# State-space decay exponents from running sums read back from HBM, in a hybrid diffusion trunk

## The chip, the cores and the metric

The kernel runs on one NeuronCore of a Trainium2 chip. Its engines work in parallel from instruction streams of their own: TensorE (PE, matrix products into PSUM), VectorE (DVE), ScalarE (ACT), GpSimd (POOL) and SyncE (SP, which here only issues DMAs). The metric is the device time of one execution in microseconds (us); lower is better. The time of the kernel before is the median of three runs, 1761.66 us (1760.66 to 1762.17).

## The reference

A two-layer trunk over 512 latent tokens of width 1024, with 256 context tokens. Layer 0 has a mixer of two parts, a Mamba-2 state-space group (SSD: 16 heads of 64 channels, two groups, state 128, both directions) and a gated linear attention group; layer 1 has a conformer convolution; both layers end in a convolutional gated MLP. The change lies in the SSD part, which for each direction computes, in chunks of 128 tokens:

```
a_cum = jnp.cumsum(a, -1)                       # a = dt * a_coef, per head
decay = jnp.exp(segsum(a))                      # exp(cs[l] - cs[s]) for s <= l, else 0
cb = jnp.einsum('bclgn,bcsgn->bgcls', cc, bc)
y_diag = jnp.einsum('bgcls,bgjcls,bcsgjp->bclgjp', cb, decay, xdt)
...
y = y_diag + y_off      # y_off: what the state at the chunk's start contributes
```

Here `xdt` is the token's value times its step size dt. The two directions are added, a skip term `d_skip * xs` comes on top, the result is multiplied by silu(z) and normalized by its root mean square in two groups of 512 channels. Inputs and weights are float32.

## The kernel before

The whole trunk is one program. Tokens lie on 128 partitions, four chunks of latent tokens and two of context. The weights are streamed in blocks of 128x512: `_wload` (L178) issues one DMA on SP (L182), ACT casts the upper half `whi` into the matmul's number format (L184), and the lower half `wlo = wraw - whi` is subtracted on DVE or, where `lo_pool` is set, on GpSimd (L188). Five blocks are loaded ahead. A projection then takes three matmuls per product: hi x hi, lo x hi, hi x lo (L214 to L216, L233 to L235).

The SSD stage is `mixer` with `dt_stage` (L510) and `ssd` (L592). `dt_stage` makes the step sizes `dt`, the decays `a`, and by matmuls with triangles of ones the running sums p1 and totals p2, whose exponentials are `ef` and `dtot`. `mixer` then runs, for each of two groups of eight heads, the convolution of that group's channels (`conv5`, L328 to L340), transposes into token order (`to_tokens`, L342), and `ssd`. The scheduler of the framework orders each engine's stream by priorities, so that matmuls of the next projections (`ps`, `psv`, `psz`) fall between those of the SSD loop; a change in the code thus moves other instructions too.

In `ssd`, after the backward states (`u`, `sb`) and the products `pcb = B C` of all four chunks, a loop runs over four chunks and in each over two halves of four heads:

- ACT multiplies the triangle masks by `a`, eight times 128x128 (`r`, L644); PE turns them into the decay exponents with two fp32 matmuls of 128x512 (`seg`, L645); ACT takes the exponential (`e`, L647).
- ACT and DVE make the weight `w`, which has both directions' dt times the masked products `cbm` (L633, L650, L651); DVE forms `e*w` (L653); four matmuls by head give `yp` (L656).
- The states' part is two matmuls `po` (L661), scaled on DVE into `yo` (L663). DVE adds skip, yp and yo into `y` and multiplies by silu(z) (L667 to L671). ACT squares and sums (L672); `sf` is carried on by `u` and DVE.

After the loop, DVE makes the root-mean-square factor in a chain of small operations (`rstd`, L588, L256 to L261) and scales `y` (L682). PSUM is shared by pools: four buffers `mm` for projections, two `lv` (seg, pcb), two `mi` (yp, po, u, transposes). A matmul into a new tile waits until the buffer's last reader is through. The attention part follows: its value projection `psv` is copied out by ACT into `v` (L496).

Of the kernel before, what the change touches and what calls it, by code (L numbers as in the profile page):

```python
# [8 lines left out]
F32 = mybir.dt.float32  # L9
F32R = mybir.dt.float32r  # L10
BF16 = mybir.dt.bfloat16
I32 = mybir.dt.int32
# [135 lines left out]
class Net:  # L148
# [193 lines left out]
    def to_tokens(self, src, dst, n, mi):  # L342

        nc = self.nc
        pt = mi.tile([P, n, P], F32, tag="mi", name="pt")
        for c in range(n):
            nc.tensor.transpose(pt[:, c, :], src[:, c * P:(c + 1) * P], self.ident)
        nc.scalar.copy(dst, pt)

    def mixer(self):  # L350
# [93 lines left out]
        sp = ss.enter_context(self.pool("ssp", 1))  # L444
        dx = self.stack()
# [3 lines left out]
        dt, a, ef, dtot, wdec = dts  # L449
        self.dump("dt", dt)  # L450
# [7 lines left out]
        for g in range(2):  # L458
# [4 lines left out]
            for i in range(4):  # L463
                ps, ps2 = self.fm(mm, "win", C_XS + (g * 4 + i) * P, act, also=actc)
                xf = self.conv5(ps, T, g * 4 + i, tmps)
                self.to_tokens(xf, y[:, :, (g * 4 + i) * P:(g * 4 + i + 1) * P], NCH, mi)
                xf2 = self.conv5(ps2, TC, g * 4 + i, tmps)
                self.to_tokens(xf2, xct[:, :, i * P:(i + 1) * P], NCC, mi)
# [4 lines left out]
            self.ssd(g, y, xct, bfm, cfm, btok, dts, rows, sz, sp, tmps, lv, mi)  # L473
# [38 lines left out]
    def dt_stage(self, act, actc, sp, sx, mm, mi, rows):  # L512
# [51 lines left out]
        dtot = sp.tile([P, 2, NC6, H], F32, name="dtot")  # L564
        nc.scalar.activation(out=ef, in_=p1, func=AF.Exp)
# [6 lines left out]
        return dt, a, ef, dtot, wdec  # L572
# [19 lines left out]
    def ssd(self, g, y, xct, bfm, cfm, btok, dts, rows, sz, sp, tmps, lv, mi):  # L592
        nc = self.nc
        dt, a, ef, dtot, wdec = dts
# [35 lines left out]
        cbm = sp.tile([P, 2, NCH, P], F32, tag="cbm", name="cbm")  # L630
        for d in range(2):
            m = (self.le, self.ge)[d]
            nc.vector.tensor_tensor(out=cbm[:, d], in0=pcb, in1=bass.AP(tensor=m.tensor, offset=m.offset, ap=[list(m.ap[0]), [0, NCH], [1, P]]), op=ALU.mult)  # L633
        ssq = tmps.tile([P, NCH], F32, tag="ssq", name="ssq")
        for c in range(NCH):
            yp = mi.tile([P, 512], F32, tag="mi", name="yp")
            for hq in range(2):
                h0 = g * GH + hq * 4
                r = tmps.tile([P, 2, 4, P], F32, tag="r", name="r", bufs=1)
                seg = lv.tile([P, 4, P], F32, tag="lv", name="seg")  # L640
                for d in range(2):
                    m = (self.le, self.ge)[d]
                    for j in range(4):
                        nc.scalar.mul(r[:, d, j, :], m, a[:, c, d, h0 + j:h0 + j + 1])  # L644
                    nc.tensor.matmul(seg, (self.gt, self.lt)[d], r[:, d], start=d == 0, stop=d == 1)  # L645
                e = tmps.tile([P, 4, P], F32, tag="e", name="e")
                nc.scalar.activation(out=e, in_=seg, func=AF.Exp)  # L647
                w = tmps.tile([P, 4, P], F32, tag="w", name="w")
                for j in range(4):
                    nc.scalar.mul(w[:, j, :], cbm[:, 1, c, :], dt[:, c, 1, h0 + j:h0 + j + 1])  # L650
                    nc.vector.scalar_tensor_tensor(out=w[:, j, :], in0=cbm[:, 0, c, :], scalar=dt[:, c, 0, h0 + j:h0 + j + 1],  # L651
                                                   in1=w[:, j, :], op0=ALU.mult, op1=ALU.add)
                nc.vector.tensor_tensor(out=e, in0=e, in1=w, op=ALU.mult)  # L653
# [12 lines left out]
            dd = rows[:, R_D - R_DTB + g * GH:R_D - R_DTB + (g + 1) * GH]  # L666
            nc.vector.tensor_tensor(out=heads(yc), in0=heads(yc), in1=bch(dd, HD), op=ALU.mult)  # L667
# [12 lines left out]
        for c in range(NCH):  # L680
            yc = y[:, c, g * 512:(g + 1) * 512]
            nc.vector.tensor_scalar_mul(yc, yc, r[:, c:c + 1])  # L682
# [567 lines left out]
```

## Time and profile before

| what | value |
|---|---|
| median of three runs | 1761.66 us |
| the profiled execution | 1762.31 us, span 1760.5 us |
| PE busy | 1707.3 us, 97% of the span |
| DVE busy | 1247.9 us, 71% |
| ACT busy | 850.5 us, 48% |
| POOL busy | 525.8 us, 30% |
| last links of the chain that ended last | PE lines L214 to L216 above all |

The profile gives for each engine the time in which it worked, and for each group of instructions count, sum and mean. A share over the whole span hides stages: GpSimd at 30% does nothing at all in the SSD stage, which lies at about 100 to 290 us of the span. So rows of that stretch count. In the timeline a row has start, length, engine, line, operation and tiles; the length of an instruction overlaps that of the next, so that distances from start to start, not lengths, are what a sequence costs.

### The profile page before, as it was taken

The numbers are of one execution on the slowest core, as the hardware profiler recorded it, in microseconds if no ns is written. First come the engines' busy times: TensorE is split into PE (matmuls) and PEld (weight loads), VectorE is DVE, ScalarE is ACT, GpSimd is POOL, SyncE is SP. The second block draws the span as 40 slices with busy tenths as digits, with TensorE's granted clock in tenths as the row PEclk, the third lists the DMA queues.
The fourth block names the chain that finished last, engine by engine and source line by source line (L and its number), as shares of the span: only waits on it lengthen the run. The fifth ranks groups of instructions, "written<-read, shape, count | busy, mean of one in ns | idle before, by whom it ended". The sixth has DMA issues, their size and how long they took to land. (4 is left out here: it accounts for less than half of the span.)

```text
span 1760.5 us, 26474 instructions
## 1 busy us (share of the span) xinstructions
PE 1707.3 (97%) x9574; PEld 1465.3 (83%) x9574; DVE 1247.9 (71%) x2368; ACT 850.5 (48%) x1713; POOL 525.8 (30%) x436
## 2 busy tenths in 40 slices
PE   6999999999999999999999999999999999999996
PEld 5987768989899987887888888988898888888886
DVE  7778988969695996378777731488788777776125
ACT  4556775354444544364333422499534743333233
POOL 4400000000000003544444444533415444444451
PEclk9999999999999999999999999999999999999998
DMA  9621102434343448423333333322203233333331
GB/s 365 239 66 48 31 19 89 135 119 154 109 144 120 133 139 277 134 85 114 108 108 108 109 112 96 102 73 60 61 26 90 85 96 98 100 96 96 96 107 61
DMA packets 92194, 194.02 MB, mean 110 GB/s; under 512 B 10496, under 2 KB 13568, under 8 KB 92064
## 3 DMA queue, kind: packets, MB, share of 16 engines
q1 hardware_dynamic: 92016, 192.21, 35.0%
q8 instruction: 75, 1.23, 0.3%
q14 instruction: 55, 0.45, 0.1%
q0 software_dynamic: 48, 0.13, 0.0%
HBM read 190.21 MB, written 2.10 MB: 109 GB/s over the span
## 5 line engine op out<-in xcount | busy, mean ns | idle before, releaser
L188 POOL TENSOR_TENSOR wlo<-wraw,whi 128x512 fp32r<-128x512 f32 x388 | 510.0, 1318 | 1188.5 <-ACT whi L184 1171.6
L184 ACT CAST whi<-wraw 128x512 fp32r<-128x512 f32 x488 | 300.9, 619 | 509.2 <-PE ps L215 254.0
L214 PE MATMUL ps<-h1hi,whi 128*128 128x512 f32 x768 | 299.9, 391 | 2.0 <-DVE acc L1066 1.9
L216 PE MATMUL ps<-h1hi,wlo 128*128 128x512 f32 x768 | 299.6, 390 | 0.6 <-POOL wlo L188 0.6
L215 PE MATMUL ps<-h1lo,whi 128*128 128x512 f32 x768 | 299.6, 390 | 0.0
L1066 DVE SCALAR_TENSOR_TENSOR acc<-ps,pcol,acc 128x441 f32<-128x441 f32 (+2 forms) x320 | 222.4, 695 | 57.5 <-ACT acc L1058 47.9
L214 PEld LDWEIGHTS ps<-h1hi,whi 128*128 128x128 f32 x768 | 144.5, 188 | 32.2 <-ACT acc L1058 2.3
L216 PEld LDWEIGHTS ps<-h1hi,wlo 128*128 128x128 f32 x768 | 144.6, 188 | 31.2 <-POOL wlo L188 1.1
L215 PEld LDWEIGHTS ps<-h1lo,whi 128*128 128x128 f32 x768 | 144.7, 188 | 29.5
L273 DVE CUSTOM_DVE_ANT_0 junk<-ada,sc,pcol 128x1024 bf16<-128x1024 f32 x80 | 105.8, 1322 | 14.8 <-DMA ada<-adaw 14.6
L903 DVE SCALAR_TENSOR_TENSOR x<-ps,mod,x 128x512 f32<-128x512 f32 x14 | 10.5, 750 | 146.7 <-PE ps L216 146.7
L215 PE MATMUL ps<-glo,whi 128*128 128x512 f32 x264 | 102.7, 389 | 0.0
L214 PE MATMUL ps<-ghi,whi 128*128 128x512 f32 x264 | 102.7, 389 | 0.0
L216 PE MATMUL ps<-ghi,wlo 128*128 128x512 f32 x264 | 102.7, 389 | 0.0
L1158 DVE SCALAR_TENSOR_TENSOR cr<-u,pcol,cr 128x511 f32<-128x511 f32 (+20 forms) x156 | 97.7, 699 | 1.7 <-ACT cr L1141 1.5
L214 PE MATMUL ps<-hhi,whi 128*128 128x512 f32 x240 | 98.0, 408 | 0.0
L215 PE MATMUL ps<-hlo,whi 128*128 128x512 f32 x240 | 96.5, 402 | 0.0
L216 PE MATMUL ps<-hhi,wlo 128*128 128x512 f32 x240 | 96.0, 400 | 0.0
L188 DVE TENSOR_TENSOR wlo<-wraw,whi 128x512 fp32r<-128x512 f32 x100 | 68.0, 686 | 26.0 <-ACT whi L184 25.2
L979 DVE TENSOR_TENSOR glo<-acc,ghi 128x512 fp32r<-128x512 f32 x44 | 56.4, 1282 | 29.7 <-ACT ghi L978 29.6
L233 PE MATMUL psz<-whi,hhi 128*128 128x256 f32 (+1 forms) x224 | 67.5, 302 | 0.0
L234 PE MATMUL psz<-wlo,hhi 128*128 128x256 f32 (+1 forms) x224 | 67.1, 300 | 0.0
(353 smaller groups left out, 4168.0 us busy)
## 6 DMA issues: line engine op xcount, KB each, us to landing
wraw<-wst SPq DMA_DIRECT2D x488, 256.0 KB, 2.7
ada<-adaw SPq DMA_DIRECT2D x104, 512.0 KB, 3.6
xk<-xT SPq DMA_DIRECT2D x8, 256.0 KB, 7.8
x<-xT SPq DMA_DIRECT2D x8, 256.0 KB, 5.1
out<-n SPq DMA_DIRECT2D x16, 128.0 KB, 1.7
xk<-ctxT SPq DMA_DIRECT2D x8, 128.0 KB, 4.0
sc<-rows SPq DMA_DIRECT2D x1, 512.0 KB, 3.5
scc<-rows SPq DMA_DIRECT2D x1, 512.0 KB, 7.6
```

The lines of the kernel that those rows point to most:

```text
L184: nc.scalar.copy(hi, raw)
L188: eng.tensor_tensor(out=lo, in0=raw, in1=hi.bitcast(F32), op=ALU.subtract)
L214: mm(ps, w[0], a[0], start=start, stop=False)
L215: mm(ps, w[0], a[1], start=False, stop=False)
L216: mm(ps, w[1], a[0], start=False, stop=stop)
L233: mm(ps, a[0], w[0], start=start, stop=False)
L234: mm(ps, a[0], w[1], start=False, stop=False)
L273: nc.vector.tensor_tensor_reduce(out=junk, in0=raw, in1=self.sc if cond is None else cond, scale=1.0, scalar=self.pc("adab", n), op0=ALU.m ...
L903: self.after = self.nc.vector.scalar_tensor_tensor(out=r, in0=ps, scalar=self.modc(layer, j, i), in1=r, op0=ALU.mult, op1=ALU.add)
L979: return nc.vector.tensor_tensor(out=lo, in0=x, in1=hi.bitcast(F32), op=ALU.subtract)
L1066: nc.vector.scalar_tensor_tensor(out=o, in0=grid(pg)[:, r0 + dy - 1:r1 + dy - 1, c0 + dx - 1:c1 + dx - 1], scalar=wcol(dy, dx), in1=o, op0 ...
L1158: nc.vector.scalar_tensor_tensor(out=acc[:, t0:t1], in0=u[:, t0 + d:t1 + d], scalar=self.pc("cdw", tap * 8 + i), in1=acc[:, t0:t1], op0=AL ...
```

## The change

The exponents no longer come from matmuls. `dt_stage` copies the running sums out of p1, transposes them on PE (`pcum`), copies them by ACT (`crow`) and writes them to a DRAM scratch `cumd` of 32 rows by 512 tokens with a DMA on ACT's queue. `nb` holds ln(dt) minus the running sum of the token on the partition. In `ssd` each (chunk, half) reads eight rows of `cumd`, each on all 128 partitions, 512 KB in pieces of 512 bytes, by ACT's queue into `r` (three buffers). ACT adds `nb` as a bias: direction 0 into `e` in SBUF, direction 1 into `seg` in PSUM. DVE copies the second over the first where the mask says "after" (copy_predicated), ACT takes one exponential, and DVE multiplies by the unmasked `cb`. The weight dt is thus in the exponent. The diagonal's second direction and the skip factor are put together in `own` (one reduction and one small operation per chunk). The scaling of `y` by the root-mean-square factor moves from DVE to ACT, and `lo_pool` is on from the end of `dt_stage` to the end of the second `ssd`.

```diff
+        self.cumd = ss.enter_context(self.pool("cumd", 1, bass.MemoryType.DRAM)).tile([2 * H, T], F32, name="cumd")
...
+        self.lo_pool = True
         for g in range(2):
...
-                self.to_tokens(xf2, xct[:, :, i * P:(i + 1) * P], NCC, mi)
+                done = self.to_tokens(xf2, xct[:, :, i * P:(i + 1) * P], NCC, mi)
...
+            self.ssd(g, y, xct, bfm, cfm, btok, dts, rows, sz, sp, tmps, lv, mi, done)
+        self.lo_pool = False
...
+        cum = sx.tile([P, NCH, H // 4, 2, 4], F32, name="cum")
+        by4 = lambda t: t.rearrange("p c (q j) -> p c q j", j=4)
+        for d in range(2):
+            nc.vector.tensor_copy(cum[:, :, :, d, :], by4(p1[:, d, 0:NCH, :]))
+        pcum = mi.tile([P, T], F32, tag="mi", name="pcum")
+        for c in range(NCH):
+            nc.tensor.transpose(pcum[:32, c * P:(c + 1) * P], cum[:, c].rearrange("p q d j -> p (q d j)"), self.ident)
+        crow = sx.tile([32, T], F32, name="crow")
+        nc.scalar.copy(crow, pcum[:32, :])
+        nc.scalar.dma_start(out=self.cumd, in_=crow)
+
+        nb = sp.tile([P, NCH, 2, H], F32, name="nb")
+        nc.vector.tensor_scalar_max(nb, dt[:, 0:NCH], 1e-30)
+        nc.scalar.activation(out=nb, in_=nb, func=AF.Ln)
+        for d in range(2):
+            nc.vector.tensor_tensor(out=by4(nb[:, :, d, :]), in0=by4(nb[:, :, d, :]), in1=cum[:, :, :, d, :], op=ALU.subtract)
...
-        cbm = sp.tile([P, 2, NCH, P], F32, tag="cbm", name="cbm")
-        for d in range(2):
-            m = (self.le, self.ge)[d]
-            nc.vector.tensor_tensor(out=cbm[:, d], in0=pcb, in1=bass.AP(tensor=m.tensor, offset=m.offset, ap=[list(m.ap[0]), [0, NCH], [1, P]]), op=ALU.mult)
+        cb = sp.tile([P, NCH, P], F32, tag="cb", name="cb")
+        nc.scalar.copy(cb, pcb)
+
+        own = sp.tile([P, NCH, GH], F32, tag="own", name="own")
+        cbd = sp.tile([P, NCH], F32, tag="cbd", name="cbd")
+        dd = rows[:, R_D - R_DTB + g * GH:R_D - R_DTB + (g + 1) * GH]
+        for c in range(NCH):
+            junk = tmps.tile([P, P], F32, tag="cj", name="cj", bufs=1)
+            nc.vector.tensor_tensor_reduce(out=junk, in0=cb[:, c, :], in1=self.ident, scale=1.0, scalar=0.0, op0=ALU.mult, op1=ALU.add,
+                                           accum_out=cbd[:, c:c + 1])
+            nc.vector.scalar_tensor_tensor(out=own[:, c, :], in0=dt[:, c, 1, g * GH:(g + 1) * GH], scalar=cbd[:, c:c + 1], in1=dd,
+                                           op0=ALU.mult, op1=ALU.add)
+        after = bass.AP(tensor=self.gt.tensor, offset=self.gt.offset, ap=[list(self.gt.ap[0]), [0, 4], [1, P]]).bitcast(I32)
...
-                r = tmps.tile([P, 2, 4, P], F32, tag="r", name="r", bufs=1)
+                r = tmps.tile([P, 2, 4, P], F32, tag="r", name="r", bufs=3)
+                cd = self.cumd[:]
+                nc.scalar.dma_start(out=r, in_=bass.AP(tensor=cd.tensor, offset=cd.offset + h0 * 2 * T + c * P, ap=[[0, P], [T, 8], [1, P]]))
+
+                e = tmps.tile([P, 4, P], F32, tag="e", name="e")
                 seg = lv.tile([P, 4, P], F32, tag="lv", name="seg")
-                for d in range(2):
-                    m = (self.le, self.ge)[d]
-                    for j in range(4):
-                        nc.scalar.mul(r[:, d, j, :], m, a[:, c, d, h0 + j:h0 + j + 1])
-                    nc.tensor.matmul(seg, (self.gt, self.lt)[d], r[:, d], start=d == 0, stop=d == 1)
-                e = tmps.tile([P, 4, P], F32, tag="e", name="e")
-                nc.scalar.activation(out=e, in_=seg, func=AF.Exp)
-                w = tmps.tile([P, 4, P], F32, tag="w", name="w")
-                for j in range(4):
-                    nc.scalar.mul(w[:, j, :], cbm[:, 1, c, :], dt[:, c, 1, h0 + j:h0 + j + 1])
-                    nc.vector.scalar_tensor_tensor(out=w[:, j, :], in0=cbm[:, 0, c, :], scalar=dt[:, c, 0, h0 + j:h0 + j + 1],
-                                                   in1=w[:, j, :], op0=ALU.mult, op1=ALU.add)
-                nc.vector.tensor_tensor(out=e, in0=e, in1=w, op=ALU.mult)
+                with self.tc.issue_after(done.ins):
+                    for d, dst in ((0, e), (1, seg)):
+                        for j in range(4):
+                            nc.scalar.activation(out=dst[:, j, :], in_=r[:, d, j, :], func=AF.Identity, bias=nb[:, c, d, h0 + j:h0 + j + 1])
+                nc.vector.copy_predicated(e, after, seg)
+                nc.scalar.activation(out=e, in_=e, func=AF.Exp)
+                nc.vector.tensor_tensor(out=e, in0=e, in1=ap(cb, c * P, [[0, 4], [1, P]]), op=ALU.mult)
...
-            nc.vector.tensor_tensor(out=heads(yc), in0=heads(yc), in1=bch(dd, HD), op=ALU.mult)
+            nc.vector.tensor_tensor(out=heads(yc), in0=heads(yc), in1=bch(own[:, c, :], HD), op=ALU.mult)
...
-            nc.vector.tensor_scalar_mul(yc, yc, r[:, c:c + 1])
+            nc.scalar.mul(yc, yc, r[:, c:c + 1])
```

The scheduler puts the new streams together anew. Three places matter here. Rows are instructions in the order of one engine: line, operation, written and read tiles with their numbers, shape, and how many alike follow each other. The lines are those of each version's own code.

On PE, at the end of the second group: before, the last chunk's yp and po matmuls are mixed with the value projection (psv).

```order
L656 MATMUL yp_2727<-y_84,e_2740 128x64 x4
L661 MATMUL po_2784<-sf_2723,cfm_100 128x512
L233 MATMUL psv_2963<-whi51_2360,chi_88 128x256
L656 MATMUL yp_2727<-y_84,e_2768 128x64 x4
L234 MATMUL psv_2963<-wlo51_2362,chi_88 128x256
L235 MATMUL psv_2963<-whi51_2360,clo_89 128x256
L233 MATMUL psv_2963<-whi51_2360,chi_88 128x256
L661 MATMUL po_2788<-sb_2442,cfm_100 128x512
L234 MATMUL psv_2963<-wlo51_2362,chi_88 128x256
```

After the change, the same place on PE (L683 is now yp, L688 po, L701 u):

```order
L701 MATMUL u_2640<-xd_2624,btok_101 128x512
L216 MATMUL ps_2919<-hhi_79,wlo53_2745 128x512
L683 MATMUL yp_2646<-y_84,e_2649 128x64 x4
L688 MATMUL po_2685<-sf_2642,cfm_100 128x512
L683 MATMUL yp_2646<-y_84,e_2668 128x64 x4
L688 MATMUL po_2689<-sb_2402,cfm_100 128x512
L214 MATMUL ps2_2920<-chi_88,whi52_2326 128x256
L215 MATMUL ps2_2920<-clo_89,whi52_2326 128x256
```

The value projection, and the latent half of the next projection (`ps_2919`), now stand ahead of the last chunk; its context half `ps2_2920` follows the last po directly.

On ACT, at the same place, before: the last exponentials, four casts of weights, the last square and sum, then the copies of the value projection.

```order
L647 ACTIVATE e_2768<-seg_2757 128x512
L184 CAST whi54_2847<-wraw54_2845 128x512
L184 CAST whi55_2853<-wraw55_2851 128x512
L184 CAST whi56_2859<-wraw56_2857 128x512
L184 CAST whi57_3021<-wraw57_3019 128x512
L672 ACTIVATE yo_2790,ssq_2489<-y_84 128x512
L496 COPY v_2838<-psv_2863 128x512
L496 COPY v_2838<-psv_2913 128x512
L496 COPY v_2838<-psv_2963 128x512
L697 ACT_TABLE_LOAD
L697 ACTIVATE f_3013<-ps_3017 128x512
```

After the change, ACT at the same place (L679 is the exponential, L698 the square, L708 the scaling of y, L499 the copies):

```order
L679 ACTIVATE e_2649<-e_2649 128x512
L698 ACTIVATE yo_2632,ssq_2462<-y_84 128x512
L679 ACTIVATE e_2668<-e_2668 128x512
L698 ACTIVATE yo_2691,ssq_2462<-y_84 128x512
L708 ACTIVATE y_84<-y_84,r_2700 128x512 x4
L499 COPY v_2740<-psv_2765 128x512
L499 COPY v_2740<-psv_2815 128x512
L499 COPY v_2740<-psv_2865 128x512
L723 ACT_TABLE_LOAD
L723 ACTIVATE f_2915<-ps_2919 128x512
```

The four scalings of y, which read the root-mean-square factor, now stand between the last square and the copies of the value projection.

On PE, at the end of the first group, before: the last chunks' matmuls with seg and projection matmuls between them.

```order
L656 MATMUL yp_1986<-y_84,e_1999 128x64 x4
L645 MATMUL seg_2016<-r_2015,tri_60 128x512
L661 MATMUL po_2043<-sf_1982,cfm_100 128x512
L645 MATMUL seg_2016<-r_2015,tri_60 128x512
L215 MATMUL ps_2184<-hlo_80,whi42_1585 128x512
L216 MATMUL ps_2184<-hhi_79,wlo42_1587 128x512
L661 MATMUL po_2047<-sb_1701,cfm_100 128x512
L214 MATMUL ps_2184<-hhi_79,whi42_1585 128x512
L215 MATMUL ps_2184<-hlo_80,whi42_1585 128x512
L656 MATMUL yp_1986<-y_84,e_2027 128x64 x4
```

After the change, PE at the end of the first group (L649 is pcb of the second group):

```order
L683 MATMUL yp_1903<-y_84,e_1906 128x64 x4
L688 MATMUL po_1944<-sf_1899,cfm_100 128x512
L688 MATMUL po_1948<-sb_1720,cfm_100 128x512
L683 MATMUL yp_1903<-y_84,e_1925 128x64 x4
L649 MATMUL pcb_2441<-cfm_100,bfm_99 128x128 x3
L701 MATMUL u_1958<-xd_1942,btok_101 128x512
L649 MATMUL pcb_2441<-cfm_100,bfm_99 128x128
L683 MATMUL yp_1964<-y_84,e_1967 128x64 x4
L688 MATMUL po_2003<-sf_1960,cfm_100 128x512
L688 MATMUL po_2007<-sb_1720,cfm_100 128x512
L683 MATMUL yp_1964<-y_84,e_1986 128x64 x4
```

The projection matmuls between the last two chunks' own matmuls are gone from here; they stand further up in PE's order.

More of the change, by code (lines that the diff above doesn't have):

```diff
@@ L347, in to_tokens @@
             nc.tensor.transpose(pt[:, c, :], src[:, c * P:(c + 1) * P], self.ident)
-        nc.scalar.copy(dst, pt)
+        return nc.scalar.copy(dst, pt)
     def mixer(self):
@@ L448, in mixer @@
         tmps = ss.enter_context(self.pool("sst", 2))
-        dt, a, ef, dtot, wdec = dts
-        self.dump("dt", dt)
+        self.dump("dt", dts[0])
+        self.lo_pool = True
         for g in range(2):
@@ L472, in mixer @@
             self.dump(f"xt{g}", y[:, :, g * 512:(g + 1) * 512])
-            self.ssd(g, y, xct, bfm, cfm, btok, dts, rows, sz, sp, tmps, lv, mi)
+            self.ssd(g, y, xct, bfm, cfm, btok, dts, rows, sz, sp, tmps, lv, mi, done)
+        self.lo_pool = False
         self.dump("y", y)
@@ L571, in dt_stage @@
             nc.vector.tensor_tensor(out=wdec[:, d, c, :], in0=wdec[:, d, c, :], in1=dtot[:, d, c2, :], op=ALU.mult)
-        return dt, a, ef, dtot, wdec
+        return dt, nb, ef, dtot, wdec
     def zproj(self, i, sz, acth, pool, tag, col=C_Z, dst=None):
@@ L590, in rstd, with ssd @@
         return r
-    def ssd(self, g, y, xct, bfm, cfm, btok, dts, rows, sz, sp, tmps, lv, mi):
+    def ssd(self, g, y, xct, bfm, cfm, btok, dts, rows, sz, sp, tmps, lv, mi, done):
         nc = self.nc
-        dt, a, ef, dtot, wdec = dts
+        dt, nb, ef, dtot, wdec = dts
         NC6 = NCH + NCC
@@ L665, in ssd @@
             yc = y[:, c, g * 512:(g + 1) * 512]
-            dd = rows[:, R_D - R_DTB + g * GH:R_D - R_DTB + (g + 1) * GH]
-            nc.vector.tensor_tensor(out=heads(yc), in0=heads(yc), in1=bch(dd, HD), op=ALU.mult)
+            nc.vector.tensor_tensor(out=heads(yc), in0=heads(yc), in1=bch(own[:, c, :], HD), op=ALU.mult)
             nc.vector.tensor_tensor(out=yc, in0=yc, in1=yp, op=ALU.add)
```

## The prediction

> **What bounds the kernel now.** I first read the busy shares by stretch in the middle of the state-space stage (microseconds from the start, length, then busy time and instruction count of each engine, granted TensorE clock, DMA share, GB/s):
>
> ```profile
> core 0: us, PE busy (x) PEld busy (x) DVE busy (x) ACT busy (x) POOL busy (x), PEclk, DMA share, GB/s
> 160.00:200.00 40.00, 40.00 (x173) 25.50 (x172) 37.05 (x74) 31.50 (x98) 0.00 (x0) 1.00 0.02 7
> 240.00:260.00 20.00, 20.00 (x96) 13.00 (x94) 18.13 (x36) 14.33 (x45) 0.00 (x0) 1.00 0.00 1
> ```
>
> TensorE (PE) is busy without a break and at full clock in both chunk loops. A busy PE can still be a stretched one, so next I take start-to-start distances from its timeline, and the group of the decay matmuls:
>
> ```profile
> L645 PE MATMUL seg<-r,tri x64: 590/592/697, 120.6 to 272.9; 128*128 128x512 f32 x64
> ...
> 155.26 1.02 PE L645 MATMUL seg<-r,tri 128*128 128x512 f32 x2
> 156.12 1.02 PE L620 MATMUL u<-xd,btok 128*128 128x512 f32 x2
> ...
> 163.01 1.00 PE L656 MATMUL yp<-y,e 128*128 128x64 f32 x8
> 163.82 0.47 PE L215 MATMUL ps<-hlo,whi 128*128 128x512 f32 x1
> ```
>
> An fp32 matmul of 512 columns leaves two records and takes 156.12 - 155.26 = 0.86 us of PE; four yp matmuls take 0.81. Added up over stretches of 20 us, the start-to-start distances of all matmuls exceed such undisturbed ones by 2 us at most, so PE sets the pace there and each matmul taken away is worth its distance. But VectorE (DVE) is close behind: 37.05 of 40 us. Its own distance for a 128x512 operation, and the costs of the groups that the change touches (count, then busy us, mean ns):
>
> ```profile
> 159.25 0.68 DVE L610 TENSOR_TENSOR ctmp<-sb,dtot 128x512 f32<-128x512 f32 x1
> 159.85 0.68 DVE L605 TENSOR_TENSOR xd<-y,wdec 128x512 f32<-128x512 f32 x1
> ...
> L644 ACT ACTIVATE r<-tri,a 128x128 f32<-128x128 f32 x128 | 39.5, 390 | 0.0
> L650 ACT ACTIVATE w<-cbm,dt 128x128 f32<-128x128 f32 x64 | 20.6, 392 | 0.0
> L651 DVE SCALAR_TENSOR_TENSOR w<-cbm,dt,w 128x128 f32<-128x128 f32 x64 | 19.9, 344 | 2.8 <-ACT w L650 2.8
> L746 DVE COPY_PREDICATED p<-msk,lev 128x512 f32<-128x512 int32 x56 | 41.4, 739 | 4.2 <-PE lev L744 2.4 <-ACT kg L741 0.4
> L188 DVE TENSOR_TENSOR wlo<-wraw,whi 128x512 fp32r<-128x512 f32 x100 | 68.0, 686 | 26.0 <-ACT whi L184 25.2
> L188 POOL TENSOR_TENSOR wlo<-wraw,whi 128x512 fp32r<-128x512 f32 x388 | 510.0, 1318 | 1188.5 <-ACT whi L184 1171.6
> ```
>
> So a DVE operation costs 0.60 us in a run, a masked copy some 0.66 (739 ns less the same overlap).
>
> **The change part by part.** I work against the profiled execution's own 1762.31 us (span 1760.5), 0.65 us above the median of 1761.66.
>
> *Removed from PE, -27.5 us.* Two seg matmuls for each of 16 (group, chunk, half): 32 x 0.86 = 27.5. The row above counts 64 records, which agrees. The order confirms that they are gone and that 24 of the 100 DVE subtractions of the weights move to GpSimd, so the change does what its words say for these two groups only.
>
> *ScalarE (ACT), hidden.* 128 r products and 64 w products go (39.5 + 20.6 = 60.1 us); 128 Identity activations come at the same 128x128 size, 128 x 0.39 = 50, with eight y scalings, two cb copies and the logarithm: some 63 in all. ACT was busy 31.50 of 40, so the total stays under PE's. DVE loses 64 x 0.31 = 20 us of w work, four mask products and 24 x 0.60 of subtractions, and gains 16 x 0.66 of masked copies and 16 small ones: about 25 us less over the stage. Where PE has spare matmuls of the projections to run, both are covered.
>
> *Preparation, +1.4 us.* Four transposes of the running sums cost PE 0.4. Their PSUM slot comes free only behind an Exp that stands behind the logarithm and a table load (1.28 us in the row below), and only two small filler matmuls stand there: about 1.0.
>
> *Where no filler is left, +10 us.* In the first group's last chunk the new PE order has no projection work: PE has four yp groups, five po or u and a half-length pcb left, 4 x 0.81 + 5 x 0.86 + 0.45 = 8.0 us, beside 19 DVE operations, 19 x 0.61 = 11.6: +3.6. Between the groups, the transposes of the convolution wait behind DVE's end of the group: seven DVE operations and one on ACT, 5.0 us, beside 3.1 of PE, then 3.8 beside 2.3: +3.3. In the second group's last part 62 x 0.602 + 8 x 0.66 = 42.6 us of DVE stand beside 39.7 of PE: +3.0. Each could be zero, if DVE is ahead when it gets there.
>
> *The end of the second group, +8.9 us.* These are the rows of the place:
>
> ```profile
> 277.44 1.02 PE L661 MATMUL po<-sb,cfm 128*128 128x512 f32 x2
> 281.40 0.40 PE L214 MATMUL ps<-hhi,whi 128*128 128x512 f32 x1
> 286.87 0.28 PE L214 MATMUL ps<-chi,whi 128*128 128x256 f32 x1
> ...
> 278.55 0.68 DVE L663 TENSOR_TENSOR yo<-po,ef 128x512 f32<-128x512 f32 x1
> 281.91 0.68 DVE L671 TENSOR_TENSOR y<-y,sz 128x512 f32<-128x512 f32 x1
> 283.72 0.16 DVE L588 TENSOR_SCALAR v<-ssq 128x4 f32<-128x4 f32 x1
> 286.09 1.68 DVE L682 TENSOR_SCALAR y<-y,r 128x512 f32<-128x512 f32 x4
> ...
> 282.69 0.63 ACT L672 ACTIVATE yo<-y 128x512 f32<-128x512 f32 x1 [0.46 <-DVE y L671]
> 283.32 1.54 ACT L496 COPY v<-psv 128x512 f32<-128x512 f32 x3
> 284.87 1.28 ACT L697 ACT_TABLE_LOAD   x1
> ```
>
> Before, PE ran the value projections (psv) and 24 more matmuls of 0.23, (286.87 - 281.40)/24, between the last po and the next context block, and the copies that free psv's slots waited for nothing but ACT. Afterwards PE has run all this earlier, in the time that the seg matmuls left; its next instruction behind the last po needs a slot that the first v copy frees, and this copy now stands on ACT behind the four y scalings, and these behind the root-mean-square chain. From the last po: four DVE operations (4 x 0.60 + 0.08 = 2.5), Square to the factor (282.59 to 286.09, 3.5), four scalings at the pace of the copies (four at 0.52, 2.1), one copy and its signal (0.8): 8.9 us with PE idle. What is queued behind them on ACT, the other copies, the table load and the first gate activation, waits too, and PE waits for the copies alone. Ends: 0, if PE reaches the place so late that all is done, and 11 with the chain's operations apart.
>
> *The clock, +1.4 us.* After the one long pause that the trace has:
>
> ```profile
> 671.96 0.39 PE L216 MATMUL psg<-ohi,wlo 128*128 128x512 f32 x1
> 675.36 1.09 PE L818 MATMUL pt<-tri,o 128*128 128x128 f32 x4 [3.02 <-DVE o L791]
> ...
> 675.00:676.00 1.00, 0.64 (x3) 0.67 (x4) 1.00 (x3) 0.00 (x0) 0.00 (x0) 0.50 0.34 33
> 676.00:677.00 1.00, 1.00 (x6) 0.82 (x5) 1.00 (x2) 0.51 (x1) 0.00 (x0) 0.50 0.74 299
> ...
> 678.00:679.00 1.00, 1.00 (x7) 0.87 (x6) 0.51 (x1) 0.97 (x2) 0.00 (x0) 0.92 1.04 256
> ```
>
> After 3.02 us of idle PE the granted clock is 0.50 until about 678.1, some 2.8 us of work at half speed: 1.4 lost. I add it once, for the end of the second group. [...]
>
> *The r reads, hidden.* Sixteen reads of 512 KB go out on ACT's queue, three buffers ahead. Rows of such reads:
>
> ```profile
> 0.74 0.38 SPq L301 DMA_DIRECT2D sc<-rows  x1
> ...
> 3.06 8.10 SPq L182 DMA_DIRECT2D wraw<-wst  x7
> ...
> ada<-adaw SPq DMA_DIRECT2D x104, 512.0 KB, 3.6
> ```
>
> They land in 3.6 us; the new order leaves 8 to 9 before the first use. The issue held its queue 0.38 for one read, and 8.10/7 = 1.16 with a full queue. No row shows a read cut into 1024 pieces of 512 bytes, issued by ACT: I take 0.38 to 1.16, hidden in ACT's slack; the far end is a rival below.
>
> *The subtractions on GpSimd.* 1318 ns each on an engine with POOL at 0.00 there: hidden, if they don't slow DVE; this is a rival too.
>
> Sum: -27.5 + 1.4 + 3.6 + 3.3 + 3.0 + 8.9 + 1.4 = -5.9, so 1762.3 - 5.9 = 1756.4; on the median's footing, 0.65 lower, **1756**.
>
> **The rivals.** *A, the loops have no waits.* DVE gets ahead in the earlier chunks and the +10 of places without filler vanish (with ends at zero): -27.5 + 1.4 + 8.9 + 1.4 = -15.8, 1746. For it: DVE loses about 25 us. Against: the last chunks' operations depend on the chunk itself.
>
> *B, GpSimd slows DVE.* These two groups of DVE operations run while GpSimd is busy (minimum, median and maximum ns):
>
> ```profile
> L979 DVE TENSOR_TENSOR glo<-acc,ghi x44: 679/1369/1371, 808.1 to 1621.9; 128x512 fp32r<-128x512 f32 x44
> ...
> L1069 DVE TENSOR_TENSOR acc<-acc,ps x42: 679/689/689, 805.8 to 1620.4; 128x512 f32<-128x512 f32 x42
> ```
>
> Operations with two SBUF inputs double, those with one input in PSUM do not. If eight subtractions meet the loop where DVE decides, each holds up one such operation by 0.69: 8 x 0.69 = 5.5, to 1762, which is no change. In the order only four or so stand in the loop beside DVE's dense part. [...]
>
> *C, slower: ACT is held by issuing the r reads.* If the hold grows with the number of pieces (1024 against 128), 0.38 x 8 = 3.0 at the far end, say 2.6 for the queue of a busy engine. Thirteen reads stand in the loops: 13 x 2.2 above the 0.38 = 29 us on ACT, which had 40 - 31.50 = 8.5 spare in 40 us, so 17 over two loops: 12 us are left over, PE waits for e: 1756 + 12 = **1768 to 1769**. It decides from a hold of about 17/13 + 0.38 = 1.7 us. For it: no row excludes it; against: full-queue issues of 1.16 were waiting for room, not for pieces.
>
> *D, the clock drops in the loops as well.* Each of two loop waits of about 3 us that come in one piece costs another 1.4: 1756 + 2.8 = 1759. This lies in the forecast's range.
>
> **How the numbers follow.** Forecast 0.50 (D inside it), A 0.17, B 0.13, C 0.15, rest 0.05. A difference under 0.2%, 3.5 us, cannot be told from no change here: same is 1758.1 to 1765.2. Of the forecast 0.36 is faster and 0.14 same (with D); A is faster; B is 0.10 same, 0.03 slower; C slower; the rest 0.02 faster, 0.03 slower. Faster 0.55, same 0.24, slower 0.21. The range goes from just under A, 1745, to C's 1769; both ends of the end-of-group term (0 and 11) fall inside.
>
> **What would show it.** The changed profile should have: no L645 rows; PE idle of 8 to 9 us once, near 270, between the last po and a context block of the projection, put down to ACT's v copies; shorter idle in the last chunk of each group, put down to DVE (copy, yo, e) and not to r; DVE's share in the loops at 0.95 or more; granted clock 0.50 for some 3 us after the long pause. A is right if PE has no gaps in the loops; B if DVE's e, xd and ctmp show means well over 690 ns; C if idle ACT or PE ends on r, or issues on ACT's queue last over 1.7 us. I would be wrong in kind if the pause at the end of the second group does not appear, or if a stage after the state-space part changes its length.

## The result and the profile after

The change makes the kernel slower: 1778.64 us (median of four, 1775.04 to 1780.08) against 1761.16 us (the three runs of the kernel before and a fourth), a ratio of 1.0098 with a 95% interval of 1.008 to 1.0115, so 17.5 us more. The forecast was 1756, with a range from 1745 to 1769. The profiled execution took 1779.14 us.

The page of the changed kernel (busy us, share of the span, instructions; then the DMA issues with KB and us to landing) has PE less busy and the span longer:

```profile
span 1777.4 us, 26295 instructions
PE 1696.9 (95%) x9514; PEld 1463.1 (82%) x9514; DVE 1235.3 (70%) x2313; ACT 840.3 (47%) x1661; POOL 557.4 (31%) x460
...
PEclk9989898999999999999999999999999999999998
...
r<-cumd ACTq DMA_DIRECT2D x16, 512.0 KB, 5.4
```

PE has 60 instructions less and the seg rows are gone, but its clock row, which was nines up to the last of its 40 slices, now has three eights in the first seven: most of the change lies before 310 us. There I added up, from the timelines of PE, every start-to-start distance and took off what the same instruction takes undisturbed (0.228 us for a 512-column projection matmul, 0.119 for one of 256 columns, 0.43 for each fp32 record of 512 columns, and so on). What is left is time lost on PE between 80 and 345 us: 5.5 us before, 50.1 after. The balance closes: 50.1 - 5.5 - 27.5 (seg) + 0.4 (transposes) = 17.5 us. The medians differ by 17.5 and the two profiled executions by 16.8; that the first agrees to the decimal is chance, since such sums to a fixed time are good to some 2 us. So the 27.5 us were really taken off PE, and some 43 to 45 us came back as pauses and slow matmuls. The pauses, on PE's timeline after (start, length, instruction; in brackets the idle time and what ended it):

```profile
103.89 0.39 PE L214 MATMUL ps<-hhi,whi 128*128 128x512 f32 x1
107.28 0.63 PE L563 MATMUL p<-a,tri 128*128 128x96 f32 x2 [3.01 <-DVE nb L581]
...
115.35 0.28 PE L216 MATMUL ps<-chi,wlo 128*128 128x256 f32 x1
118.31 0.76 PE L214 MATMUL ps<-hhi,whi 128*128 128x512 f32 x1 [2.67 <-DVE cacc L336]
118.87 0.63 PE L215 MATMUL ps<-hlo,whi 128*128 128x512 f32 x1
119.30 0.63 PE L216 MATMUL ps<-hhi,wlo 128*128 128x512 f32 x1
...
205.62 1.26 PE L683 MATMUL yp<-y,e 128*128 128x64 f32 x8 [2.50 <-DVE e L680]
...
217.15 0.76 PE L214 MATMUL ps<-hhi,whi 128*128 128x512 f32 x1 [3.48 <-DVE cacc L336]
...
284.93 1.97 PE L683 MATMUL yp<-y,e 128*128 128x64 f32 x8 [3.57 <-DVE e L680]
...
290.10 1.87 PE L688 MATMUL po<-sb,cfm 128*128 128x512 f32 x2
301.19 0.58 PE L214 MATMUL ps<-chi,whi 128*128 128x256 f32 x1 [9.21 <-ACT v L499]
```

Six pauses of 2.5 us or more, where the kernel before has none in this stretch. The rows after a pause show the second loss: from 118.87 to 119.30 a projection matmul takes 0.43 us instead of 0.23. The busy shares in stretches of 1 us say why (the number behind POOL is the granted clock), one stretch behind each of five places:

```profile
core 0: us, PE busy (x) PEld busy (x) DVE busy (x) ACT busy (x) POOL busy (x), PEclk, DMA share, GB/s
108.00:109.00 1.00, 1.00 (x7) 1.00 (x6) 0.00 (x0) 0.92 (x1) 0.00 (x0) 0.50 0.00 0
119.00:120.00 1.00, 1.00 (x4) 0.80 (x3) 1.00 (x2) 0.99 (x3) 0.00 (x0) 0.50 0.95 253
211.00:212.00 1.00, 1.00 (x5) 0.82 (x5) 0.90 (x2) 0.50 (x1) 0.00 (x0) 0.50 0.92 150
288.00:289.00 1.00, 1.00 (x4) 0.49 (x3) 0.25 (x1) 0.00 (x0) 0.00 (x0) 0.50 0.62 227
303.00:304.00 1.00, 1.00 (x7) 1.00 (x6) 0.00 (x0) 0.99 (x3) 0.00 (x0) 0.50 0.00 0
```

Half clock with PE busy. Over all such stretches, busy time times (1 - granted clock) adds up to 14.5 us; before it is zero from 90 to 330 us. By place:

| place in the trace after | lost on PE | of it half clock | forecast |
|---|---|---|---|
| preparation, 100 to 126 us | 10.5 | 4.7 | 1.4 |
| up to the first group's last chunk, 126 to 197 | 3.9 (before: 2) | 0 | 0 |
| end of the first group, 197 to 222 | 13.4 | 4.4 | 6.9 |
| second group up to its last chunk, 222 to 280 | 1.7 (as before) | 0 | 0 |
| second group, last chunk, 280 to 290 | 6.3 | 3.4, with the end of po | 3.0 |
| behind its last po, 290 to 345 | 14.3 | 2.0 | 8.9 + 1.4 |

What made the first pause, on the timeline of DVE and of GpSimd after:

```profile
98.08 5.30 POOL L188 TENSOR_TENSOR wlo<-wraw,whi 128x512 fp32r<-128x512 f32 x4 [8.53 <-ACT whi L184]
...
99.63 1.34 DVE L544 TENSOR_TENSOR dte<-dtz 128x192 f32<-128x192 f32 x1
101.00 1.23 DVE L545 TENSOR_SCALAR dtp<-dte 128x192 f32<-128x192 f32 x1
102.27 3.69 DVE L547 SCALAR_TENSOR_TENSOR dtp<-dtp,dte 128x192 f32<-128x192 f32 x7
```

and the same three operations before:

```profile
100.15 0.35 DVE L541 TENSOR_TENSOR dte<-dtz 128x192 f32<-128x192 f32 x1
...
101.02 0.25 DVE L542 TENSOR_SCALAR dtp<-dte 128x192 f32<-128x192 f32 x1
...
101.80 2.71 DVE L544 SCALAR_TENSOR_TENSOR dtp<-dtp,dte 128x192 f32<-128x192 f32 x7
```

The four subtractions that GpSimd now runs lie beside the chain that makes dt, and these operations of the chain take 1.34 + 1.23 + 3.69 = 6.3 us instead of 3.3. PE waits for the end of this chain, the decays `a` (the bracket names the next DVE instruction). But before, the four subtractions stood between the operations of the chain, on DVE itself, so the end of the chain comes later by less than that:

```profile
105.33 0.36 DVE L552 SCALAR_TENSOR_TENSOR a<-dt,ea 128x192 f32<-128x192 f32 x1
...
105.83 0.43 PE L560 MATMUL p<-a,tri 128*128 128x96 f32 x2
```

These are `a` and p1 before. After the change `a` is made here:

```profile
106.78 0.36 DVE L555 SCALAR_TENSOR_TENSOR a<-dt,ea 128x192 f32<-128x192 f32 x1
```

The same work of PE starts at 100.10 before and at 100.46 after, so `a` is 1.45 - 0.36 = 1.1 us late. The other 1.9 us of the pause are PE's own order: from that start 24 projection matmuls of 512 columns stood ahead of p1 before, and only 16 after (with one of 256 columns less: 8 x 0.228 + 0.12 = 1.9).

The second pause is ACT's doing, on its timeline after:

```profile
107.31 0.31 ACT L582 ACTIVATE nb<-nb 128x128 f32<-128x128 f32 x1 [4.80 <-DVE nb L581]
107.64 1.28 ACT L586 ACT_TABLE_LOAD   x1
...
111.41 0.58 ACT L577 COPY crow<-pcum 32x512 f32<-32x512 f32 x1 [0.61 <-PE pcum L575]
112.02 0.36 ACTq L578 DMA_DIRECT2D cumd<-crow  x1
114.16 0.62 ACT L184 CAST whi<-wraw 128x512 fp32r<-128x512 f32 x1 [2.17 <-PE ps L215]
114.68 1.02 ACT L332 ACTIVATE cacc<-ps,pcol 128x256 f32<-128x256 f32 x2
...
115.62 0.38 ACTq L670 DMA_DIRECT2D r<-cumd  x1
...
298.11 2.56 ACT L708 ACTIVATE y<-y,r 128x512 f32<-128x512 f32 x4 [2.41 <-DVE r L261]
300.57 1.53 ACT L499 COPY v<-psv 128x512 f32<-128x512 f32 x3
```

The first taps of the context convolutions (L332), which the kernel before ran at 100.75, stand behind the logarithm, the copy and the write of the running sums (and a weight cast that waits 2.17 us for PE) and start at 114.68; they free nothing until DVE has run the remaining taps, and those hold the PSUM buffers of the next projection. At the end of the second group the four scalings and then the v copies run as forecast. Issuing an r read held ACT's queue 0.37 or 0.38 us, once 0.98; PE waits for such a read nowhere, and ACT twice, 0.90 and 0.20 us.

### The profile page after: what moved, and what is told of

The parts are those of the page before. It is cut to its first block, busy times and chain, and to the rows that moved or that the text cites. A ratio compares the mean times of both kernels' runs of the same rounds, so it can differ in the third digit from the quotient of the medians.

```text
span 1777.4 us, 26295 instructions
## 1 busy us (share of the span) xinstructions
PE 1696.9 (95%) x9514; PEld 1463.1 (82%) x9514; DVE 1235.3 (70%) x2313; ACT 840.3 (47%) x1661; POOL 557.4 (31%) x460
## 3 DMA queue, kind: packets, MB, share of 16 engines
q8 instruction: 75, 1.23, 0.3%
## 5 line engine op out<-in xcount | busy, mean ns | idle before, releaser
L188 POOL TENSOR_TENSOR wlo<-wraw,whi 128x512 fp32r<-128x512 f32 x412 | 541.6, 1319 | 1173.5 <-ACT whi L184 679.8
L929 DVE SCALAR_TENSOR_TENSOR x<-ps,mod,x 128x512 f32<-128x512 f32 x14 | 10.5, 750 | 146.7 <-PE ps L216 146.7
L1005 DVE TENSOR_TENSOR glo<-acc,ghi 128x512 fp32r<-128x512 f32 x44 | 56.0, 1273 | 29.1 <-ACT ghi L1004 29.0
L214 PE MATMUL ps<-chi,whi 128*128 128x256 f32 x208 | 60.9, 293 | 9.2 <-ACT v L499 9.2
L188 DVE TENSOR_TENSOR wlo<-wraw,whi 128x512 fp32r<-128x512 f32 x76 | 52.1, 689 | 22.0 <-ACT whi L184 21.9
```

Source lines behind the costliest of these rows:

```text
L188: eng.tensor_tensor(out=lo, in0=raw, in1=hi.bitcast(F32), op=ALU.subtract)
L214: mm(ps, w[0], a[0], start=start, stop=False)
L929: self.after = self.nc.vector.scalar_tensor_tensor(out=r, in0=ps, scalar=self.modc(layer, j, i), in1=r, op0=ALU.mult, op1=ALU.add)
L1005: return nc.vector.tensor_tensor(out=lo, in0=x, in1=hi.bitcast(F32), op=ALU.subtract)
```

## The experiments

Theory 1: each loss is a pause that one wait makes, plus half clock behind it. Theory 2: GpSimd's subtractions slow DVE, and that is the main cost. Each run was timed against the kernel before on its own chip, so ratios are compared; 0.1% is 1.8 us. Between two executions of unchanged code the first 100 us differ by some 3 us (p1 starts at 110.07 in the first run below and at 107.28 after), so the time lost on PE is the finer measure of the two. Here it is worked out as above, but between two places that every version has: from the first matmul of dt's projection (at 85 to 88 us) to the last group of `lev` matmuls before the pause of 1.4 us that every trace has at 617 to 642 us. The column gives what is lost there beyond the kernel before.

| run | ratio to before, interval | more lost on PE than before, us | half clock from 80 to 345, us |
|---|---|---|---|
| the changed kernel | 1.0098 (1.008 to 1.0115) | 42.9 | 14.5 |
| y scaled on DVE | 1.0078 (1.0049 to 1.0107) | 38.1 | 12.9 |
| subtractions on DVE | 1.0053 (1.0033 to 1.0074) | 35.4 | 12.5 |
| before, subtractions on GpSimd | 1.0045 (1.0028 to 1.0063) | 8.1 | 1.7 |
| before, y scaled on ACT | 1.0014 (0.9999 to 1.0029) | 3.5 | 1.7 |
| exponents alone | 1.0016 (1.0006 to 1.0027) | 29.1 | 11.0 |
| and sums later | 1.0012 (0.9998 to 1.0026) | 29.1 | 9.2 |
| and three e | 0.9991 (0.9981 to 1.0001) | 25.7 | 8.2 |
| and last square on DVE | 0.9953 (0.9935 to 0.9971) | 17.7 | 3.9 |
| and filled pauses | 0.9953 (0.994 to 0.9966) | 9.2 | 4.3 |
| changed, pauses filled | 1.0064 (1.0048 to 1.008) | 20.3 | 5.1 |
| changed, GpSimd later | 1.0063 (1.0048 to 1.0078) | 36.9 | 7.9 |
| three e, GpSimd later | 1.0004 (0.9992 to 1.0016) | 28.0 | 6.7 |

**The scaling of y back on DVE.**

```diff
-            nc.scalar.mul(yc, yc, r[:, c:c + 1])
+            nc.vector.tensor_scalar_mul(yc, yc, r[:, c:c + 1])
```

> The changed kernel with only the scaling of y back on DVE. Theory 1 (single pauses of PE, each made by one wait, plus half clock after each): the 9.2 us pause before the context block ends when the last square is through instead of behind the factor and four scalings; in the changed trace the square ends at 295.7 and the first v copy starts at 300.57, so the pause shrinks by 4.9 to about 4.3, the half clock after it stays, all other pauses stay: 1778.6 - 4.9 = 1773.7. Theory 2 (GpSimd's subtractions slow DVE and that is the main cost): the pause is not the main cost, but the edit would give the same 4.9. Theory 3 (the wait is only passed on to the first gate activation and then to PE): the time stays at 1777 to 1779.

The pause went as theory 1 has it, on PE's timeline of this run:

```profile
293.45 1.08 PE L688 MATMUL po<-sb,cfm 128*128 128x512 f32 x2
299.18 0.58 PE L214 MATMUL ps<-chi,whi 128*128 128x256 f32 x1 [4.66 <-ACT v L499]
```

4.66 us instead of 9.21, and 4.8 us less are lost on PE, where theory 1 expected 4.9. The ratio fell by 0.2%, some 3.5 us, with an interval too wide to tell 3.5 from none; the first 100 us of this execution were 2.8 us longer. The trace, not the time, speaks against the third theory: the wait was not passed on in full.

**All subtractions back on DVE.**

```diff
         self.dump("dt", dts[0])
-
-        self.lo_pool = True
```

> The changed kernel with all 24 subtractions back on DVE. Theory 1: only the chain of dt gets shorter, by some 1.5 us (a at 106.8 instead of 105.3); the pause there falls from 3.0 to 1.5, too short to lower the clock, another 1.6 less; against this DVE has 24 x 0.6 more in places where it decides, perhaps 3 to 8 us: 1774 to 1783. Theory 2: the doubled operations vanish in the chunk loops too and the time falls by 8 or more, to 1770 or less.

The ratio fell by 0.45%, 7.9 us, and 7.5 us less are lost on PE. That lies between the two theories: the pause before p1 is gone altogether, and the pause at the convolution's buffers grows to 4.14. So GpSimd costs more than the 1.5 us I gave to theory 1, but the other pauses stay: it isn't the main cost.

**The kernel before with the subtractions on GpSimd.** The same two lines that switch it on and off, in the old kernel.

> The kernel before, with only the 24 subtractions on GpSimd (the diff's one part alone). Theory 1: the chain of dt gets 1.5 us longer in front of waiting matmuls, DVE is otherwise relieved: 1760 to 1765. Theory 2: doubled DVE operations while PE is just covered cost more, 1768 or above.

Slower by 0.45%, 1770.7 by the ratio: the time that theory 2 gave, but the place is theory 1's. PE loses 8.1 us more, of which a pause of 3.00 us before p1 and the half clock behind it, 1.7, are the largest piece. PE's order has the same 16 matmuls of 512 columns ahead of p1 here as the changed kernel, so the edit brings both parts of that pause, the late `a` and the order. This edit alone, then, costs 5 to 11 us, in a kernel that had DVE just under PE.

**The kernel before with y scaled on ACT.**

```diff
-            nc.vector.tensor_scalar_mul(yc, yc, r[:, c:c + 1])
+            nc.scalar.mul(yc, yc, r[:, c:c + 1])
```

> The kernel before, with only the scaling of y moved to ACT. Theory 1: the four scalings stand ahead of ACT's v copies, which then wait for the factor; PE has 26 + 24 matmuls of other work there, about 9.4 us, so little or nothing shows: 1760 to 1763. If the pause at the end of the second group came from this edit by itself, 1766 to 1770.

1.0014, 2.5 us, within its interval of none: near what theory 1 expected. On PE's timeline of this run the wait shows, but small, since 50 other matmuls stand in front of it:

```profile
286.64 0.39 PE L216 MATMUL ps<-hhi,wlo 128*128 128x512 f32 x1
289.18 0.39 PE L214 MATMUL ps<-chi,whi 128*128 128x256 f32 x1 [2.15 <-ACT v L496]
```

The same edit costs 9.21 - 4.66 = 4.6 us of pause where the new order has used those matmuls up, and 2.15 where it has not.

**The exponents alone**: both undone in the changed kernel.

> The changed kernel with both side edits undone (scaling of y and all subtractions back on DVE): the new exponents alone. Theory 1 (single pauses of PE and half clock after each): the gains of the two runs before add up, about 3.5 us for the scaling and 8 for the subtractions against the kernel before, so from 17.5 over it to about 6 over it; the pauses at the convolution's PSUM slots (4.1 us) and in the last chunk of each group (about 5 and 5) stay, and so the 27.5 us taken from PE are still more than given back. Rival (without the side edits the exponents do what they should): 15 us or more below the kernel before.

1.0016, 2.8 us over the kernel before, against 6 expected; the rival's 15 below is out. Even the core of the change, with 27.5 us taken off PE, is no gain: 29.1 us come back.

**The running sums later.** The transposes, the copy, the write and `nb` (the code from `pcum` on) move out of `dt_stage` into a function of their own, called behind the context convolutions:

```diff
             self.to_tokens(bcf, btok[:, g, NCH:, :], NCC, mi)
+        dts = self.sums(dts, sp, mi)
```

> The run before it, with the transposes of the running sums, the copy, the write and the logarithm moved behind the context convolutions of B, so that ACT's first taps of those convolutions no longer stand behind them. Theory 1: the pause of 4.1 us before the first x projection and the half clock behind it, some 2.5, go: 6 us below the run before it. Rival (the pause is DVE's chain of taps, which comes late whatever ACT does): within 2 us of it.

Where I looked, theory 1 was right: the pause before the first x projection falls from 4.14 to 0.69 us, and with it the half clock behind it. The time does not follow: 1.0012 against 1.0016, and the lost time is the same 29.1, since the new order has pauses of 3.86 (for `cfm`, at 195) and 4.56 (behind the first group) in place of smaller ones. Expected 6, got 1 at most: the mechanism is shown, its worth is not.

**Three buffers for e**, in addition:

```diff
-                e = tmps.tile([P, 4, P], F32, tag="e", name="e")
+                e = tmps.tile([P, 4, P], F32, tag="e", name="e", bufs=3)
```

> The run with the sums later, and with three buffers for e in place of two, so that the exponent chain can run ahead by one more half chunk. Theory 1 (in the last chunks DVE's sheer amount of work is what PE waits for): within 2 us of the run with the sums later. Rival (the chain waits for a free e): the pauses of the last chunk of both groups shrink by 2 us or more each and the time falls by 4 or more.

0.2% less, 3.7 us, between the two: pauses of 2.38 instead of 2.51 in the second group's last chunk, others moved. Unclear as to the reason, but it is level with the kernel before.

**The last square on DVE**, in addition:

```diff
-            nc.scalar.activation(out=offs[1], in_=yc, func=AF.Square, accum_out=ssq[:, c:c + 1])
+            if g == 1 and c == NCH - 1:
+                nc.vector.tensor_tensor_reduce(out=offs[1], in0=yc, in1=yc, scale=1.0, scalar=0.0, op0=ALU.mult, op1=ALU.add,
+                                               accum_out=ssq[:, c:c + 1])
+            else:
+                nc.scalar.activation(out=offs[1], in_=yc, func=AF.Square, accum_out=ssq[:, c:c + 1])
```

> The run with three buffers for e, and with the last square and sum of the second group on DVE instead of ACT. In that run PE waits 5.3 us for ACT's first v copy, which stands behind this square. Theory 1: the copies now follow the last exponential, the pause goes to below 1 us and the half clock behind it (1.9 us lost) with it: 6 to 7 us less, about 7 us below the kernel before. Rival (the wait passes on to the first gate activation, or the added DVE operation delays the factor and what follows): within 2 us of the run before it.

Right in mechanism and size: 0.9953 against 0.9991, 6.7 us, on a single instruction that stood in front of the v copies. PE's timeline of this run at the place of the 9.21 us pause:

```profile
276.23 1.12 PE L693 MATMUL po<-sb,cfm 128*128 128x512 f32 x2
278.03 0.39 PE L214 MATMUL ps<-chi,whi 128*128 128x256 f32 x1 [0.68 <-ACT v L498]
```

This version is faster than both: 8.3 us below the kernel before (0.9953, interval 0.9935 to 0.9971). The kernel before was not run with the square on DVE, so how much of the 8.3 us is owed to the new exponents is not shown.

**Filled pauses.** To see what the clock costs apart from the wait, matmuls whose result nobody reads go into the pauses of the changed kernel, 20 of them, 17.2 us of PE work more:

```diff
+            if c >= NCH - 2:
+                wm = lv.tile([P, 512], F32, tag="lv", name="wm")
+                for j in range(8 if c == NCH - 1 and g else 4):
+                    nc.tensor.matmul(wm, e[:, j % 4, :], sb[:, c, :], start=True, stop=True)
             yc = y[:, c, g * 512:(g + 1) * 512]
```

> The changed kernel with matmuls whose result nobody reads put on PE in the last two chunks of each group: four of 0.86 us each time, eight in the very last, 20 in all or 17.2 us of added PE work. Theory 1: they fall into pauses, so the pauses before the yp of the last chunk and before the context block end at the same time as before but with the clock at 1.00 behind them; the half clock from 285 to 291.6 and from 301 to 306 (3.4 and 2.1 us lost) goes, and part of the 4.4 lost at the first group's end; the time falls by 4 to 8 us although PE does 17 us more. Rival (the half clock costs nothing, since PE waits for DVE there anyway): the time stays or rises by up to 5.

1.0064 against 1.0098: with 17.2 us more to do on PE, the kernel is 6.0 us faster. The stretches of the second group's last chunk in this run:

```profile
core 0: us, PE busy (x) PEld busy (x) DVE busy (x) ACT busy (x) POOL busy (x), PEclk, DMA share, GB/s
285.00:286.00 1.00, 0.85 (x2) 0.48 (x3) 0.69 (x2) 0.00 (x0) 0.00 (x0) 1.00 0.40 51
287.00:288.00 1.00, 1.00 (x5) 0.52 (x4) 0.85 (x3) 0.00 (x0) 0.00 (x0) 1.00 0.00 0
```

Full clock, where the changed kernel had 0.50. The half clock over the whole stage falls from 14.5 to 5.1 us; what is left lies in the preparation, which was not filled, and behind the last po, where a pause of 2.78 us remained. The rival's time, as before or longer, did not come. The order of the first group's end shifted as well, so how much of the 6 us is the clock's stays open.

The same idea on the fastest version, with 12 such matmuls in the third chunk of each group and the last of the first:

> The run with the last square on DVE, and with four matmuls that nobody reads in the third chunk of each group and the last of the first group, 12 in all, 10.3 us of PE work. Theory 1 (half clock behind pauses over some 2.5 us): it gives back about as much as it adds where the pauses are filled, and the clock at the first group's end (some 6 us lost) and in the last chunk is 1.00: 2 to 5 us faster than without. Rival: slower by 3 to 10, since part of the work lies outside pauses.

No change by the ratio (0.9953 both), although 10.3 us of work were added; PE's lost time fell by 8.5. It neither gains nor costs: about break-even, not the 2 to 5 us expected. The half clock in this version at the end of the first group stays at 4.3 us.

**GpSimd only behind the context convolutions**, in the changed kernel: the four subtractions beside the dt chain stay on DVE.

```diff
-        self.lo_pool = True
...
             self.to_tokens(bcf, btok[:, g, NCH:, :], NCC, mi)
+        self.lo_pool = True
```

> The changed kernel, with the subtractions on GpSimd only from behind the context convolutions of B: the first four, which run beside the dt chain, stay on DVE, the other 20 go to GpSimd. Theory 1 (it is the dt chain alone that GpSimd slows): the pause before p1 falls from 3.0 to 0 and no half clock follows, as with all subtractions on DVE; 5 to 8 us less than the changed kernel, 9 to 12 over the kernel before. Theory 2 (GpSimd slows DVE in the chunk loops as well): no more than 2 us less.

1.0063, 6.2 us less than the changed kernel: as theory 1 has it. The pause before p1 is 1.18 us instead of 3.01 (0 was expected), and no half clock follows it. Most of GpSimd's cost is four of its 24 subtractions. The same in the version with three e:

> The run with three buffers for e, with the subtractions on GpSimd from behind the sums on (20 of 24). Theory 1: DVE has 12 us less to do where it decides in the last chunks: 2 to 4 us less than that run. Theory 2 (doubled DVE operations): 2 to 6 us more.

Here the numbers lean to theory 2: 1.0004 against 0.9991, though the intervals overlap, and 2.3 us more lost on PE. The 20 later subtractions on GpSimd at least bring no gain. In the trace of this run six 128x512 operations of DVE between 120 and 310 us take 1.3 to 1.8 us (two xd, three y, one e); in the run with three e alone none takes over 0.9.

## Why the prediction was wrong

Two terms of the sum failed: the preparation and the clock, and the clock's loss also stands inside the places behind the pauses.

*Removed from PE, -27.5 us.* Right: the balance of PE's lost time closes on it.

*Totals of ACT and DVE, hidden.* Right as totals, and beside the point. It was the place of single instructions in ACT's and DVE's order that counted.

*Preparation, +1.4.* Failed: 10.5. I priced the added transposes and one slot, and missed three things. The subtractions handed to GpSimd begin beside the dt chain (I counted the rival only in the chunk loop), and hold up its operations, 0.35 us becoming 1.34; the chain ends 1.1 us late. With them PE's order changes, and 1.9 us less of projection work stands ahead of p1. And the logarithm, copy and write went ahead of the first convolution taps on ACT, 14 us late, so that PSUM buffers were not free. The run with the subtractions off removes the first two, the run with the sums later the third.

*Where no filler is left, +10.* The waits were about as I worked them out, the loss was not: 13.4 + 6.3 = 19.7 us, of which 7.8 are half clock, and the rest, 11.9, is near the 9.9.

*The end of the second group, +8.9.* Right: 9.21 us of pause, for the v copies behind four scalings; the runs with the scaling and the square moved took it away piece by piece.

*The clock, +1.4.* Failed, and by most: 14.5, which the figures of the places contain. I counted one drop, behind the longest pause, and two more under rival D, which I priced at 2.8 and which was right in kind. The trace has six pauses of 2.5 to 9.2 us; behind two of them the half clock lasted 3.41 us, as in the one I took as a model, and behind four 6.83 or 10.24. I had the row that should have warned me, 3.02 us of idle with half clock behind it, and had forecast waits of 3.0 to 3.6 us myself without giving each its price.

*The r reads, hidden.* Right: the issue held the queue 0.38 us, once 0.98, and the reads landed in 5.4 us; rival C fell. Nor is the 1.16 us a hold: in the trace before, the seven issues of that row took 0.33 to 0.67 us each, and 4.3 us of its 8.10 went on SP's waits for a landed `wraw` (2.3) and for `wlo` (2.0). Rival B, GpSimd, was right in kind, with the wrong place: from 120 to 310 us only four 128x512 operations of DVE took over 0.9 us (1.12 to 1.75). Its reading by inputs rests on little: of the 42 `acc` in its second row only two lay wholly beside work of GpSimd, at 686 and 689 ns, and 38 beside none; and in the dt chain the `dtp<-dte` operation, with one input tile, took 1.23 us beside GpSimd instead of 0.25. Rival A fell: the waits in the last chunks came.

Sum: the terms missed are 10.5 - 1.4 in the preparation, 19.7 - 9.9 at the groups' ends, 2 at the start of the first group and 14.3 - 10.3 less 2 as before at the end: 23 us between -5.9 and +17.5.

## What to carry to other kernels

Work taken off the busiest engine is a gain only as long as other work is left that fills its waits: here 27.5 us went and the kernel got 17.5 us slower; the projections moved up into the hole, and the chain of the last chunk stood alone. (No run puts those projections back; this is read from PE's order and the filled pauses.) Where a change makes pauses on PE, count each one of 2 us and more twice, once for the wait and once for the half clock that may come with it: between 90 and 330 us of these traces 40 of 45 such pauses had one to four stretches of 3.41 us at half clock in or behind them, the shortest 2.07 us long, and five of 2.28 to 3.01 us had none. An instruction put ahead of an ACT copy that frees a PSUM buffer costs what stands behind that buffer (9.21 us of pause here, 4.66 without the four scalings): look for the copies first, then place the rest.

## What was not expected of the hardware

How long PE has to pause for the clock to drop is not settled by the length alone. In the kernel before with y scaled on ACT, 2.15 us were enough; in the run with y scaled on DVE, 3.01 us before p1 were not, in the same code that drops the clock in the changed kernel. The place of the pause counts as well. In all fourteen traces the granted clock changes only at times that are multiples of 3.41 us apart. Cut at these times, the changed kernel looks like this (start and end, length, PE busy; the granted clock is the number ahead of the last two):

```profile
103.96:107.37 3.41, 0.40 (x3) 0.12 (x2) 3.04 (x10) 0.06 (x1) 0.00 (x0) 1.00 0.32 106
107.37:110.79 3.42, 3.42 (x15) 3.00 (x16) 0.69 (x4) 2.24 (x4) 0.00 (x0) 0.50 0.00 0
...
114.20:117.61 3.41, 1.44 (x12) 1.22 (x11) 2.33 (x6) 3.41 (x6) 1.28 (x1) 1.00 0.14 44
117.61:121.03 3.42, 2.72 (x7) 2.17 (x8) 3.42 (x7) 2.01 (x3) 1.28 (x1) 0.50 0.77 211
121.03:124.44 3.41, 3.41 (x12) 2.72 (x11) 3.10 (x5) 0.58 (x2) 0.00 (x0) 0.50 0.73 187
```

The kernel before with y scaled on ACT, at its pause of 2.15 us:

```profile
286.07:289.48 3.41, 1.26 (x7) 0.76 (x6) 0.00 (x0) 3.38 (x6) 0.00 (x0) 1.00 1.00 372
289.48:292.89 3.41, 3.41 (x18) 3.41 (x17) 0.86 (x2) 3.38 (x6) 0.00 (x0) 0.50 0.10 41
```

And the run with y scaled on DVE, at its pause of 3.01 us:

```profile
105.24:108.65 3.41, 1.83 (x9) 1.17 (x7) 3.20 (x7) 0.06 (x1) 0.94 (x1) 1.00 0.63 190
108.65:112.06 3.41, 1.99 (x14) 1.64 (x14) 1.93 (x9) 1.93 (x4) 0.00 (x0) 1.00 0.01 3
112.06:115.48 3.42, 3.42 (x24) 3.08 (x24) 0.71 (x5) 0.95 (x2) 0.00 (x0) 1.00 0.09 22
```

A stretch in which PE was busy for 0.40, 1.44 or 1.26 us of 3.41 is followed by one at half clock. The 3.01 us pause that did nothing is cut in two by a border, and PE is busy for 1.83 and 1.99 us on its two sides. Over all fourteen traces, from 90 to 340 us, each of the 40 drops follows a stretch with PE busy for at most 0.52 of it; of the 909 stretches at full clock with another behind them, one was less busy than that (0.47). Elsewhere in the traces 16 of 88 drops follow busier stretches, up to 0.73, so the busy share of the profile does not settle every drop. But it shows how the same pause can cost its half clock in one execution and not in the next: its place among the borders differs.

The way back is by stretches too. From 90 to 340 us the clock returned behind 40 stretches with PE busy for 0.84 or more, and stayed at half behind 32 with 0.81 or less; at 674.75 in the kernel before it returned behind one of 0.82. The pause at 118.31 cost two stretches, and PE was busy for 0.80 of the first. Four more stayed at half though the profile has PE busy for 0.97 or more of them, one of these at 284.87 in the changed kernel; this stays open.
